# S5 loads issued by SyncE instead of GpSimd, and the tables read in two halves

## The chip, the cores and the metric

The kernel runs on one core of a Trainium2 chip, in one launch. A core has five engines that run their own instruction streams and meet at semaphores: TensorE (PE; its weight loads are shown apart as PEld), VectorE (DVE), ScalarE (ACT), GpSimd (POOL) and SyncE (SP). Transfers between HBM and the on-chip memory SBUF are issued by one of these engines and carried by 16 DMA engines that all of them share. In this kernel SyncE issues nearly all transfers, on a hardware queue; GpSimd issues some, on a software queue; ScalarE issues a few. The metric is the device time of one execution in microseconds.

## The reference

A trunk of two layers over a sequence of 1024 positions and 1024 channels, all in float32. Layer 0 has a gated DeltaNet mixer, layer 1 an S5 state-space mixer; both run beside a cross-attention of 4 heads into 256 memory tokens, and both are followed by layer norms and an MLP of 4096. The change touches only the S5 mixer of layer 1:

```python
def s5_scan(u, abar_re, abar_im, bbar_re, bbar_im, c_re, c_im):
    """h_t = Abar h_{t-1} + Bbar u_t per group; y_t = Re(C h_t). u (B,L,H) float32."""
...
def s5_mixer(x, w_in, ...):
    proj = x @ w_in
    u, xq = jnp.split(proj, [S5_DIM], axis=-1)
    ...
    y = s5_scan(u, abar_re, abar_im, bbar_re, bbar_im, c_re, c_im)
    y = y + d_skip * u
    zg = jax.nn.gelu(y)
    out = zg * jax.nn.sigmoid(zg @ w_glu + b_glu)
    return out, xq
```

There are 64 groups of 16 channels; each drives one complex state of 64 values.

## The kernel before

Large products are done in three passes of float32r halves (`mm3`, L386 to L391): every operand is split into a high part, by a cast on ScalarE, and the rest, by a subtraction on VectorE. Weights come from HBM through two buffers called raw (`load_raw`, L357; `load_split`, L362 to L370, where the issue is L359, the cast L368 and the subtraction L369).

The S5 mixer treats eight steps of time as one column, so that the scan runs over 128 columns. While layer 0's MLP runs, a side job (`s5_side`) prepares everything that doesn't depend on the activations and writes it to HBM: the rotation tables (`tabd`: a cosine table and two sine tables of opposite sign), the driving matrices (`g1d`), the reading matrices (`h1d`) and the local responses (`zd`). These stores are issued by GpSimd and stay there.

`s5_front` (L2184) then runs layer 1's mixer. It interleaves, by a string of steps, eight blocks m = 0 to 7 of eight groups each with the keys and values of the memory (wkr, wvr), the projections u (wur) and queries (wqr), the attention, and the gated unit (wgr). For a block:

- `s5_u` (L1986) projects u and writes it to `ud`; `s5_drive` loads it back as part of the tile s5t (L2040), in another layout.
- `s5_driving` (L2005), one block ahead, loads for each of two halves b of the block a matrix G1 (L2002, 256 KB) and two tables tab (L2016, 256 KB each). The first table is the cosine table, read twice by a broadcast into the lower and the upper 64 partitions. The second has one sine table in the lower 64 partitions and the other in the upper 64.
- `s5_drive` (L2034) multiplies u by G1 on TensorE (p, L2053), rotates by the tables, scans and rotates back on VectorE, with copies that swap halves on ScalarE (L2047, L2048).
- `s5_reading` (L2021) loads two matrices H1 (L2002, 256 KB each, read in runs of 512 bytes) and, through `s5_local` (L2031), the local responses M0 from `zd` (512 KB in runs of 512 bytes), into s5t, or into the tile ml for m = 7.
- `s5_read` (L2071) forms py on TensorE (L2078, L2079), applies the gelu and stores `yd` (L2082, two stores of 256 KB), which the gated unit reads again as zg (L2100).

All loads of G1, H1, tab and M0 are issued by GpSimd, 72 in all. GpSimd also computes one small power per layer norm (L512), between two VectorE instructions (L511, L519).

What sets the order: at the end of the program a planner, `settle` (L58), takes all instructions with their dependencies and puts the instructions of every engine in a fixed order, by a list schedule with estimated costs (`price`, L295), keyed to the order that TensorE's work was written in. An issue has an estimate that depends on the engine, and a transfer one that depends on its shape. Each engine then works through its own list in order, and an instruction that waits holds up all behind it on that engine. The framework also gives the transfers of the hardware queue eight semaphores in turn, so a transfer issued by SyncE waits until the one eight places before it has landed; the software queue of GpSimd has eight semaphores of its own.

Of the kernel before, what the change touches and what calls it, by code (L numbers as in the profile page):

```python
# [16 lines left out]
P = 128  # L17
# [13 lines left out]
class Trunk:  # L31
# [1967 lines left out]

    def s5_load(self, nm, tag, src):  # L2000
        t = self.tile(tag, [P, 4, P], F32, nm)
        self.nc.gpsimd.dma_start(t, src)  # L2002
        return t

    def s5_driving(self, m):  # L2005

        out = []
        for b in range(2):
            gs = slice(4 * b, 4 * b + 4)
            G1 = self.s5_load("G1", "h1", self.g1d[m, :, gs])  # L2010
            c, q = (2 * m + b) % 8, m // 4
            tabs = []
            for x in range(2):
                t = self.tile("h2", [P, 4, P], F32, "tab")
                src = self.tabd[1:3, c, q] if x else self.tabd[0, c, q].unsqueeze(0).to_broadcast([2, 64, 4, P])
                self.nc.gpsimd.dma_start(t.rearrange("p g t -> p (g t)"), src.rearrange("k p g t -> k p (g t)"))  # L2016
                tabs.append(t)
            out.append((G1, tabs))
        return out
# [7 lines left out]
    def s5_local(self, m, o):  # L2027

        M0 = o.rearrange("p (g x) -> p g x", g=8)
        z = self.zd[m]  # L2030
        self.nc.gpsimd.dma_start(M0, bass.AP(z.tensor, z.offset, [[16, 8], [8 * 240, 16], [240, 8], [1, P]]))  # L2031
        return M0

    def s5_drive(self, m, loads):  # L2034
# [447 lines left out]
```

## Time and profile before

| | us |
|---|---|
| time before, median of 3 runs | 2498.58 (2492.67 to 2499.19) |
| the profiled execution's own time | 2495.45 |
| its span, first to last instruction | 2493.7 |
| TensorE busy | 2461.7 |
| GpSimd busy | 283.7 |

The span is about 1.8 us shorter than the time of the same execution. The stage of the change lies between about 1309 us, where the load of ml is issued, and 1602 us, where the last load of H1 is. In rows of groups, a line is the line of the kernel, "out<-in" are the program's tile names without their numbers (so G is G1 and H is H1), and "xN" is the count; then come busy time, mean ns of one, and the idle time of the engine just before them with what ended it. A row of the timeline has the start in us, the length in us, engine, line, operation and tiles, and in square brackets the idle time before it. SPq is SyncE's queue of issues.

### The profile page before, as it was taken

To read this page: it belongs to the slowest core of one execution; us is meant where nothing else is said; L and a number is where in the kernel's file an instruction comes from. 1 tells how busy PE (TensorE), PEld (TensorE's weight loads), DVE (VectorE), ACT (ScalarE), POOL (GpSimd) and SP (SyncE) were. 2 spreads that over 40 slices of the span, in tenths; PEclk is the share of its full clock that TensorE was granted. 3 is DMA by queue.
4 is the path that set the end of the run, shared out by engine and by line. 5 is a ranking of instruction groups with operands and counts; after the bars stand their busy time and mean duration, and the time that the engine had idled before them with its cause. 6 is when DMAs were issued, how large, how long until landed. Compare 5 with 4: busy or idle time off the path is not lost. (4 is left out here: it accounts for less than half of the span.)

```text
span 2493.7 us, 37109 instructions
## 1 busy us (share of the span) xinstructions
PE 2461.7 (99%) x12589; PEld 2043.5 (82%) x12589; DVE 1928.7 (77%) x3629; ACT 1385.4 (56%) x3091; POOL 283.7 (11%) x405
## 2 busy tenths in 40 slices
PE   9999999999999999999999999999999999999998
PEld 7888888887787888788888888888887888888886
DVE  7776868685889987879988856683988655588777
ACT  7766677755557575554444255662466555544443
POOL 1111212110001011312120122100010000000001
PEclk9999999999999999999999999999999999999999
DMA  6544445556335665587455499874137544673422
GB/s 205 130 121 147 134 142 146 167 157 209 106 125 176 212 225 182 175 281 250 140 168 158 141 247 224 206 257 153 57 124 240 176 154 152 208 275 101 148 88 98
DMA packets 292047, 424.12 MB, mean 170 GB/s; under 512 B 120032, under 2 KB 137392, under 8 KB 291856
## 3 DMA queue, kind: packets, MB, share of 16 engines
q1 hardware_dynamic: 257520, 370.40, 46.2%
q0 software_dynamic: 31744, 46.76, 7.3%
q10 hardware_dynamic: 2592, 4.59, 0.5%
q8 instruction: 99, 1.62, 0.3%
q14 instruction: 92, 0.75, 0.1%
HBM read 285.74 MB, written 135.76 MB: 169 GB/s over the span
## 5 line engine op out<-in xcount | busy, mean ns | idle before, releaser
L389 PE MATMUL q<-wkh,hkh 128*128 128x512 f32 x784 | 306.0, 390 | 0.0
L390 PE MATMUL q<-wkl,hkh 128*128 128x512 f32 x784 | 305.7, 390 | 0.0
L391 PE MATMUL q<-wkh,hkl 128*128 128x512 f32 x784 | 305.3, 389 | 0.0
L857 ACT CAST wkh<-wr 128x512 fp32r<-128x512 f32 x168 | 104.9, 624 | 238.0 <-PE q L390 156.5
L389 PEld LDWEIGHTS q<-wkh,hkh 128*128 128x128 f32 x784 | 147.2, 188 | 31.7 <-ACT wkh L857 1.0
L391 PEld LDWEIGHTS q<-wkh,hkl 128*128 128x128 f32 x784 | 147.2, 188 | 30.5
L390 PEld LDWEIGHTS q<-wkl,hkh 128*128 128x128 f32 x784 | 147.2, 188 | 30.0
L858 DVE TENSOR_TENSOR wkl<-wr,wkh 128x512 fp32r<-128x512 f32 x168 | 115.8, 689 | 64.0 <-issue 50.9
L389 PE MATMUL wi<-xTh,wih 128*128 128x512 f32 x376 | 151.8, 404 | 1.6 <-ACT wih L368 1.6
L391 PE MATMUL wi<-xTh,wil 128*128 128x512 f32 x376 | 150.0, 399 | 0.3 <-DVE wil L369 0.3
L390 PE MATMUL wi<-xTl,wih 128*128 128x512 f32 x376 | 150.1, 399 | 0.0
L512 POOL TENSOR_TENSOR mv<-mv,mhalf 128x1 f32<-128x1 f32 x32 | 32.1, 1004 | 981.0 <-DVE mv L506 936.4
L858 DVE TENSOR_TENSOR hkl<-hr,hkh 128x512 fp32r<-128x512 f32 x196 | 134.2, 685 | 2.8 <-ACT hkh L857 2.7
L857 ACT CAST hkh<-hr 128x512 fp32r<-128x512 f32 x196 | 121.3, 619 | 4.0 <-DMA hr<-hd 4.0
L389 PE MATMUL o<-ow,ok 128*128 128x512 f32 x256 | 101.4, 396 | 1.2 <-ACT ok L1733 1.0
L391 PE MATMUL o<-ow,ok 128*128 128x512 f32 x256 | 101.5, 396 | 0.2
L390 PE MATMUL o<-ow,ok 128*128 128x512 f32 x256 | 100.2, 391 | 0.1
L850 DVE TENSOR_TENSOR y<-q,y 128x512 f32<-128x512 f32 x136 | 88.0, 683 | 0.0
L389 PEld LDWEIGHTS wi<-xTh,wih 128*128 128x128 f32 x376 | 71.2, 189 | 15.2 <-ACT wih L368 1.8
L391 PEld LDWEIGHTS wi<-xTh,wil 128*128 128x128 f32 x376 | 71.2, 189 | 14.4 <-DVE wil L369 1.0
L390 PEld LDWEIGHTS wi<-xTl,wih 128*128 128x128 f32 x376 | 71.3, 190 | 12.5
L1733 ACT CAST ok<-os 128x512 fp32r<-128x512 f32 x56 | 34.8, 623 | 54.8 <-PE o L391 41.1
(619 smaller groups left out, 7287.7 us busy)
## 6 DMA issues: line engine op xcount, KB each, us to landing
hr<-hd SPq DMA_DIRECT2D x212, 256.0 KB, 2.7
wr<-in_w_dram SPq DMA_DIRECT2D x56, 512.0 KB, 5.0
hd<-u SPq DMA_DIRECT2D x100, 256.0 KB, 2.2
w1r<-in_w_dram SPq DMA_DIRECT2D x48, 512.0 KB, 3.7
hd<-hid SPq DMA_DIRECT2D x60, 256.0 KB, 2.1
hd<-p SPq DMA_DIRECT2D x60, 256.0 KB, 2.6
w1r<-in_w_dram SPq DMA_DIRECT2D x48, 256.0 KB, 3.2
wir<-in_w_in_dram SPq DMA_DIRECT2D x23, 512.0 KB, 4.3
```

The lines of the kernel that those rows point to most:

```text
L389: mm(ps, a[0], b[0], start=start, stop=False, skip_group_check=onto)
L390: mm(ps, a[0], b[1], start=False, stop=False, skip_group_check=onto)
L391: mm(ps, a[1], b[0], start=False, stop=stop, skip_group_check=onto)
L512: nc.gpsimd.tensor_tensor(mv[:, 3:4], mv[:, 2:3], self.mhalf[:, 0:1], op=ALU.pow)
L850: V.tensor_tensor(o, bank[t], o, op=ALU.add)
L857: nc.scalar.copy(hi, s)
L858: nc.vector.tensor_tensor(lo, s, f32(hi), op=ALU.subtract)
L1733: nc.scalar.copy(hi, s)
```

## The change

`s5_load` and `s5_local` issue on SyncE instead of GpSimd. In `s5_driving`, each table is read by two transfers of 64 partitions (128 KB) on SyncE, one per half, instead of one transfer of 128 partitions (256 KB) on GpSimd: `tabd[0]` twice for the first table, `tabd[1]` and `tabd[2]` for the second. The bytes are the same. The stores of the side job, the products and the tiles are unchanged.

```diff
     def s5_load(self, nm, tag, src):
         t = self.tile(tag, [P, 4, P], F32, nm)
-        self.nc.gpsimd.dma_start(t, src)
+        self.nc.sync.dma_start(t, src)
         return t
...
             for x in range(2):
                 t = self.tile("h2", [P, 4, P], F32, "tab")
-                src = self.tabd[1:3, c, q] if x else self.tabd[0, c, q].unsqueeze(0).to_broadcast([2, 64, 4, P])
-                self.nc.gpsimd.dma_start(t.rearrange("p g t -> p (g t)"), src.rearrange("k p g t -> k p (g t)"))
+                for k in range(2):
+                    self.nc.sync.dma_start(t[64 * k:64 * k + 64], self.tabd[x * (1 + k), c, q])
                 tabs.append(t)
...
         z = self.zd[m]
-        self.nc.gpsimd.dma_start(M0, bass.AP(z.tensor, z.offset, [[16, 8], [8 * 240, 16], [240, 8], [1, P]]))
+        self.nc.sync.dma_start(M0, bass.AP(z.tensor, z.offset, [[16, 8], [8 * 240, 16], [240, 8], [1, P]]))
```

What the planner makes of it: on TensorE, VectorE and ScalarE every row stands where it stood, with the same line, operation and tile name; only the last numbers of some names, which count the program's instructions, differ. This is TensorE's order at the first products of the S5 drive (p), between two products of the memory's keys (mk), before:

```order
L390 MATMUL mk_15046<-meml_15003,wkh_15042 128x256
L391 MATMUL mk_15046<-memh_15002,wkl_15043 128x256
L2053 MATMUL p_2822_15086<-s5t_14839,G_2816_15073 128x128 x4
L2053 MATMUL p_2826_15108<-s5t_14839,G_2819_15079 128x128 x4
L389 MATMUL mk_15153<-memh_14990,wkh_15149 128x256
```

and now, at the same place of TensorE's list:

```order
L390 MATMUL mk_15046<-meml_15003,wkh_15042 128x256
L391 MATMUL mk_15046<-memh_15002,wkl_15043 128x256
L2053 MATMUL p_2822_15090<-s5t_14839,G_2816_15073 128x128 x4
L2053 MATMUL p_2826_15112<-s5t_14839,G_2819_15081 128x128 x4
L389 MATMUL mk_15161<-memh_14990,wkh_15157 128x256
```

Nothing moved there. On SyncE the loads stand between its own transfers. These are SyncE's rows from a weight to the second yd store behind it in the middle of the stage (wur and wqr are weights, ud and yd the stores, s5t<-ud the load of u), before:

```order
L359 DMA wur_15616<-in_w_in_dram 128x1024
L2082 DMA yd<-zg_15464 128x512
L2082 DMA yd<-zg_15476 128x512
L2040 DMA s5t_14839<-ud 128x1024
L359 DMA wur_15822<-in_w_in_dram 128x1024
L359 DMA wqr_16027<-in_w_in_dram 128x1024
L1997 DMA ud<-s5t_14839 128x8x128
L359 DMA wur_16062<-in_w_in_dram 128x1024
```

and now the piece from the second matrix G1 to the same last weight (its first row of G1, two yd stores and the load of M0 stand just ahead):

```order
L2002 DMA G_2899_15544<-g1d 128x512
L2002 DMA H_2902_15553<-h1d 128x4x128
L2002 DMA H_2903_15555<-h1d 128x4x128
L2040 DMA s5t_14839<-ud 128x1024
L359 DMA wur_15842<-in_w_in_dram 128x1024
L359 DMA wqr_16051<-in_w_in_dram 128x1024
L2016 DMA tab_15765<-tabd 64x512 x2
L2016 DMA tab_15770<-tabd 64x512 x2
L2016 DMA tab_15773<-tabd 64x512 x2
L2016 DMA tab_15972<-tabd 64x512 x2
L1997 DMA ud<-s5t_14839 128x8x128
L359 DMA wur_16086<-in_w_in_dram 128x1024
```

The five loads of M0, G1 and H1 come ahead of the load of u, and the eight half tables between the weights and the store of u. On GpSimd the loads stood between the powers of the layer norms (mv), here for the last three rows of the norm that ends layer 0, before:

```order
L512 TENSOR_TENSOR mv_14740<-mv_14740,mhalf 128x1
L2016 DMA tab_15077<-tabd 128x1x512
L2016 DMA tab_15081<-tabd 128x1x512
L2016 DMA tab_15083<-tabd 128x1x512
L2016 DMA tab_15132<-tabd 128x1x512
L2016 DMA tab_15134<-tabd 128x1x512
L2002 DMA G_2819_15079<-g1d 128x512
L512 TENSOR_TENSOR mv_14792<-mv_14792,mhalf 128x1
L2016 DMA tab_15138<-tabd 128x1x512
L2016 DMA tab_15140<-tabd 128x1x512
L2016 DMA tab_15343<-tabd 128x1x512
L512 TENSOR_TENSOR mv_14830<-mv_14830,mhalf 128x1
```

and now the same powers and the first of the next norm follow each other:

```order
L512 TENSOR_TENSOR mv_14740<-mv_14740,mhalf 128x1
L512 TENSOR_TENSOR mv_14792<-mv_14792,mhalf 128x1
L512 TENSOR_TENSOR mv_14830<-mv_14830,mhalf 128x1
L512 TENSOR_TENSOR mv_18512<-mv_18512,mhalf 128x1
L512 TENSOR_TENSOR mv_18566<-mv_18566,mhalf 128x1
```

GpSimd keeps no transfer in this stage; SyncE's list grows from 1299 to 1403 transfers.

## The prediction

> **What bounds the kernel now.** I read the page's busy times first, then the stage that the change touches, then the waits in it, then the DMA. The first row of the page says what the time is made of.
>
> ```profile
> PE 2461.7 (99%) x12589; PEld 2043.5 (82%) x12589; DVE 1928.7 (77%) x3629; ACT 1385.4 (56%) x3091; POOL 283.7 (11%) x405
> ```
>
> TensorE is busy for 2461.7 of 2493.7 us; only what makes it idle, or gives it more work, moves the end. The loads that change queue are issued from 1309 to 1602 us. Next comes the row of the busy times between 1400 and 1650 us, and the waits of TensorE in that stretch (in total, times, longest).
>
> ```profile
> core 0: us, PE busy (x) PEld busy (x) DVE busy (x) ACT busy (x) POOL busy (x), PEclk, DMA share, GB/s
> 1400.00:1650.00 250.00, 247.42 (x1406) 214.36 (x1405) 171.61 (x328) 136.37 (x243) 57.26 (x73) 1.00 0.86 221
> ...
> PE pv L389 <- ACT pTh L1611: 1.3, 3, 0.9
> PE mk L391 <- DVE wkl L369: 0.4, 1, 0.4
> PE wu L389 <- ACT xTh L540: 0.3, 1, 0.3
> PE pv L390 <- DVE pTl L1612: 0.2, 1, 0.2
> PE wu L390 <- DVE xTl L541: 0.2, 1, 0.2
> ```
>
> TensorE is idle for 250.00 - 247.42 = 2.6 us of 250, at full granted clock (1.00), and every named wait is for ScalarE or VectorE; none is for a transfer. So transfers that land earlier can win at most 2.6 us here, and only if one stands behind such a wait. The largest, for the attention probabilities pTh, comes after transposes of TensorE's own: no load is in it. wkl is the split of a weight that SyncE already loads.
>
> **What the change moves.** First the order of work. TensorE, VectorE and ScalarE hold the same instructions in the same order before and after, tile numbers aside, so TensorE gets no other work and no other sequence of shapes. That term is 0. Only SyncE and GpSimd change.
>
> GpSimd loses 72 transfers. These are its groups between 1300 and 1620 us (busy, mean ns of one, idle before).
>
> ```profile
> L2016 POOL DMA_DIRECT2D tab<-tabd x32 | 25.9, 815 | 106.9 <-DVE y L850 55.5 <-DVE t L2064 36.2 <-DVE r L2065 10.1
> L2002 POOL DMA_DIRECT2D H<-h1d x16 | 12.4, 793 | 4.5 <-DVE t L2064 4.5
> L2031 POOL DMA_DIRECT2D s5t<-zd x7 | 9.3, 1325 | 81.6 <-PE py L2079 56.5 <-ACT kv L1545 25.1
> L2002 POOL DMA_DIRECT2D G<-g1d x16 | 9.2, 585 | 0.0
> L2031 POOL DMA_DIRECT2D ml<-zd x1 | 1.4, 1368 | 1.1 <-DVE G1T L1925 1.1
> ```
>
> That removes 25.9 + 12.4 + 9.3 + 9.2 + 1.4 = 58.2 us from an engine that is 11% busy. It matters only where other work of GpSimd stands behind these issues: the powers of the layer norms (L512). One did, as its timeline and VectorE's wait show.
>
> ```profile
> 1411.15 3.17 POOL L2016 DMA_DIRECT2D tab<-tabd  x4 [0.57 <-PE tm L390]
> 1414.28 0.63 POOL L2002 DMA_DIRECT2D G<-g1d  x1
> 1414.88 0.61 POOL L512 TENSOR_TENSOR mv<-mv,mhalf 128x1 f32<-128x1 f32 x1
> ...
> 1413.33 0.15 DVE L511 TENSOR_SCALAR mv<-mv 128x1 f32<-128x1 f32 x1
> 1415.53 1.28 DVE L519 SCALAR_TENSOR_TENSOR y<-y,mv,gb 128x1024 f32<-128x1024 f32 x1 [0.91 <-POOL mv L512]
> ...
> 1427.01 1.04 PE L531 MATMUL xt<-ident,y 128*128 128x128 f32 x8
> 1428.34 0.49 PE L389 MATMUL wu<-xTh,wuh 128*128 128x512 f32 x1 [0.29 <-ACT xTh L540]
> ...
> 1427.21 0.59 ACT L1991 COPY s5t<-wu 128x512 f32<-128x512 f32 x1 [0.16 <-PE wu L391]
> 1427.69 1.08 ACT L540 CAST xTh<-xt 128x512 fp32r<-128x512 f32 x2
> ```
>
> VectorE was done at 1413.48; the power started 1.40 us later, behind five issues, and VectorE stood for 0.91 us. With those issues gone, this row of y is up to 0.91 us earlier. Does it reach TensorE? The next wait there, 0.29 us at 1428.34, is for the cast of xT, which ScalarE begins at 1427.69, after a copy that itself waited for TensorE's own product (0.16, PE wu). The transposes at 1427.01 had no wait. So the 0.91 us ends in VectorE's slack. I take 0; bounds 0 and -0.5 us (0.29 + 0.2, the two wu waits above).
>
> SyncE gains 104 issues: 64 half tables and 40 others. One of its issues takes 0.33 us by the wvr row below, so 104 x 0.33 = 34 us over the 300 us, and what shares the engine is only other issues. That costs nothing unless issues wait for each other, which is the real question.
>
> ```profile
> L359 SPq DMA_DIRECT2D wvr<-in_wv_dram x4: 327/330/530, 1451.1 to 1475.2; - x4
> L368 ACT CAST wvh<-wvr x4: 1047/1048/1053, 1461.0 to 1486.5; 128x1024 fp32r<-128x1024 f32 x4
> DMA to landing us min/median/max: 9.6/10.5/11.7
> ...
> L389 PE MATMUL mv<-wvh,memh x16: 389/389/476, 1470.0 to 1496.6; 128*128 128x512 f32 x16
> ...
> L2031 POOL DMA_DIRECT2D s5t<-zd x7: 1315/1324/1344, 1446.6 to 1593.1; - x7
> ```
>
> Each moved load brings its wait along, and on SyncE others queue behind it: behind a waiting zd load two yd stores, two G, two H, the load of s5t and then a weight. This is the second such place; the number in brackets is GpSimd's idle time.
>
> ```profile
> 1468.24 1.24 SPq L2082 DMA_DIRECT2D yd<-zg  x2
> 1475.20 0.33 SPq L359 DMA_DIRECT2D wvr<-in_wv_dram  x1
> ...
> 1468.93 1.32 POOL L2031 DMA_DIRECT2D s5t<-zd  x1 [7.34 <-PE py L2079]
> ```
>
> The zd load is free at 1468.9, when SyncE has its yd stores in hand, and the weight behind is due at 1475.2: eight issues of 0.33 us end by 1471.6. So the wait holds a store back by some 0.7 us (1468.93 - 1468.24) and no weight; I take 0. Without that cover a weight would be late by the whole 7.34 us. The first moved load, ml, now stands ahead of the last MLP weights at 1309 us: one issue, and 512 KB, 1.3 us at the rate found below. TensorE has no wait for a weight there (between 1300 and 1700 us it has only the five above), so 0 again.
>
> Weights lead their use: the first wvr is issued at 1451.1, cast at 1461.0, split in some 2.3 us, and used at 1470.0. That leaves 9.0 - 2.3 = 6.7 us of lead, although it took about 10 us to land. How long will loads take on SyncE's queue? The trace has no such load there, so I bound it: near, SyncE's own 256 KB loads; far, what GpSimd's queue needed.
>
> ```profile
> hr<-hd SPq DMA_DIRECT2D x212, 256.0 KB, 2.7
> tab<-tabd POOLq DMA_DIRECT2D x32, 256.0 KB, 11.9
> zg<-yd SPq DMA_DIRECT2D x16, 256.0 KB, 4.5
> ...
> GB/s 307 149 138 323 435 307 154 195 205 297 348 166 75 127 348 195 61 51 51 41 51 61 51 72 307 358 317 287 72 51 51 51 20 0 0 31 420 410 410 41
> ...
> GB/s 0 0 0 31 154 276 276 297 230 159 133 195 338 410 410 410 410 394 405 379 384 374 369 405 410 405 410 410 399 399 399 405 405 405 410 399 353 277 261 404
> ```
>
> The two rows of GB/s are slices of 0.4 us. The first spans 1364 to 1380 us, where one table and one G, 512 KB together, are alone but for two of SyncE's transfers: they end in a tail of about 51 GB/s. The second spans 1656 to 1672 us, where SyncE loads 256 KB pieces back to back at about 405. So 51 is an eighth of the full rate, and that tail, not SyncE, makes the 9 to 12 us of the moved loads. I take SyncE's rate, since the pieces are of the same 128 partitions and 2 KB rows as hr, and 4.5 us for one load (zg, short runs as H and zd have). Bounds: 2.7 and 11.9 us.
>
> The Trainium skill, page "DMA: Bandwidth & Descriptors", section "Why a DMA increments its semaphore by 16 and not by 1", says that a transfer uses the largest number of engines up to 16 that divides the outermost dimension of both sides. The old table's source has an outermost dimension of 2, so 2 engines; each half has 64, so 16. The trace agrees for the old form (51 of 405 GB/s is two engines of sixteen); no run yet shows the halves. By it the tables alone would land in SyncE's usual time, and the sum stays 0.
>
> **Sum.** 0 for order, 0 for GpSimd's relief, 0 for SyncE's issues, 0 for earlier landings: the profiled execution's own 2495.45 us stays. That execution is one of four seen (2492.67, 2495.45, 2498.58, 2499.19) and 3.1 below the median of the three runs, 2498.58; the middle of the four is (2495.45 + 2498.58) / 2 = 2497.0, and that is my time.
>
> **Rivals.**
>
> *The one queue chokes (slower).* Every transfer on SyncE's queue waits until the eighth before it has landed; GpSimd had eight places of its own. In the changed order one block of eight channel groups, from one zd load to the next, holds 20 transfers of together 5632 KB (zd 512, two yd, two G and two H of 256, s5t and ud 512 each, three weights of 512, eight half tables of 128). The row of s5t<-zd above gives the period: (1593.1 - 1446.6) / 6 = 24.4 us. Eight in flight and 20 per 24.4 us allow a latency of 8 x 24.4 / 20 = 9.8 us. Fixed time is about 2.7 - 0.26 / 0.405 = 2.1 us; eight mean pieces of 0.288 MB are 2.3 MB, 5.7 us at 405 GB/s, 7.8 us in all: it holds, by 2 us. It breaks below 2.3 / (9.8 - 2.1) = 0.30 MB per us.
>
> ```profile
> q1 hardware_dynamic: 257520, 370.40, 46.2%
> q0 software_dynamic: 31744, 46.76, 7.3%
> ```
>
> For it: over the whole run the hardware queue moved 370.40 MB in 46.2% of the span, 321 GB/s, not far above 300; GpSimd's queue 46.76 MB in 7.3%, 257 GB/s. If the moved patterns hold their 257 on the new queue, eight take 2.1 + 8.9 = 11.0 us, a period 27.5 us, 3.1 more, seven times 22 us, less the lead of 6.7: +15 us, **2512**. TensorE would then wait at wu and wq for casts whose weights are late. Against it: those averages contain two queues sharing engines, and the stretch 1400 to 1650 needs only 221 GB/s. Chance 0.08.
>
> The Trainium skill, same page, section "Queues, rings and completion order", says that each engine takes turns between the queues that have work, packet by packet; on one queue the weights lose their own turn and stand behind all tables issued before them. That speaks for this rival. The trace shows the sharing, not the single queue: the wvr loads took 10.5 us beside GpSimd's, so which of the two is worse stays open until the run.
>
> *All waits of the stage go (faster).* If late loads delayed ScalarE and VectorE in ways the waits don't name, up to 2.6 us go: 2497.0 - 2.6 = **2494.4**. Against it: the five waits above follow from the order of casts. Chance 0.12; it is still within 0.3%.
>
> *It does not do what it says.* The planner could have put the loads elsewhere; the rows of the order settle that it has not, so I give it no chance of its own.
>
> **How the numbers follow.** 0.3% of this kernel, 7.5 us, is about what a measurement can tell from no change. Forecast "no change" 0.75 at 2497.0; faster rival 0.12; slower rival 0.08; the remaining 0.05 is for a gain above 7.5 us by something that I don't see, since it would need three times TensorE's idle time here. So faster 0.05, same 0.75 + 0.12 = 0.87, slower 0.08. The range starts at the lowest run less the idle time, 2492.67 - 2.6 = 2490, and ends at the highest plus one period's loss of the slower rival, 2499.19 + 3.1 = about 2503; it leaves out the choked queue and the unseen gain.
>
> **What would show it.** Right: the tables land in 3 to 6 us instead of 11.9, TensorE's busy time between 1400 and 1650 stays within 3 us of 247.42, its waits are still for pTh, wkl and xTh, and VectorE's 0.91 us wait for L512 is gone. Wrong: waits of TensorE for wuh, wqh or G, ScalarE's casts waiting for landings, or SyncE waiting in sum for landings rather than for engines; or a stage whose TensorE work is shorter, which nothing here explains.

## The result and the profile after

| | before | after | ratio, 95% interval |
|---|---|---|---|
| first comparison, 19 runs each, us | 2496.64 (2492.67 to 2501.96) | 2491.74 (2488.68 to 2493.66) | 0.9982 (0.9976 to 0.9988) |
| second, 23 and 11 runs | 2497.47 (2493.89 to 2503.25) | 2493.14 (2491.06 to 2495.74) | 0.9979 (0.9971 to 0.9988) |
| third, 34 and 11 runs | 2499.76 (2493.43 to 2505.36) | 2493.70 (2492.49 to 2497.73) | 0.9979 (0.9969 to 0.9988) |

The changed kernel is 4 to 6 us faster, about 0.2%. That is less than the 0.3% that the prediction counts as a difference, but three comparisons agree on it, so it is real. The ranges differ too: those of before are about twice as wide (9.3, 9.4 and 11.9 us against 5.0, 4.7 and 5.2; only the first two are of equally many runs). The kernel before loses something that isn't lost in every execution.

The first profile after shows nothing of that. Its busy times and DMA queues, from the page (queue, packets, MB, share of 16 engines):

```profile
PE 2460.2 (99%) x12589; PEld 2042.3 (82%) x12589; DVE 1928.3 (77%) x3629; ACT 1383.7 (56%) x3091; POOL 224.0 (9%) x333
...
q1 hardware_dynamic: 281648, 391.38, 49.5%
q0 software_dynamic: 10112, 25.64, 3.3%
```

The stage from 1400 to 1650 us by busy times (columns as before), and below it TensorE's waits in it:

```profile
1400.00:1650.00 250.00, 247.46 (x1406) 214.45 (x1406) 171.65 (x327) 135.94 (x242) 3.05 (x4) 1.00 0.78 220
```

```profile
PE pv L389 <- ACT pTh L1611: 1.1, 2, 0.9
PE mk L391 <- DVE wkl L369: 0.4, 1, 0.4
PE wu L389 <- ACT xTh L540: 0.3, 1, 0.3
```

TensorE was busy for 247.42 us there and is now busy for 247.46, with the same waits. GpSimd went from 57.26 us to 3.05, and the DMA engines' share fell from 0.86 to 0.78 at the same 220 GB/s. By these two profiles the stage is worth nothing. Yet the profiled execution of before ran in 2495.45 us, 1.2 below the median of its 19 runs, and that of after in 2493.66, the highest of its 19: a good execution of the one was compared with a poor one of the other. So the question of the study: what does the kernel before lose in its other executions, and which part of the change stops it?

To place a loss, the table of stretches below takes the matmuls of two traces one by one (12589 in each), since TensorE's order is the same: how much later than in the first profile after does TensorE get from one matmul to another? That is worked out from the traces, and given in us by stretches of time.

### The profile page after: what moved, and what is told of

It reads as the page before. It is cut to its first block, busy times and chain, and to the rows that moved or that the text cites. A ratio compares the mean times of both kernels' runs of the same rounds, so it can differ in the third digit from the quotient of the medians.

```text
span 2491.9 us, 37103 instructions
## 1 busy us (share of the span) xinstructions
PE 2460.2 (99%) x12589; PEld 2042.3 (82%) x12589; DVE 1928.3 (77%) x3629; ACT 1383.7 (56%) x3091; POOL 224.0 (9%) x333
## 3 DMA queue, kind: packets, MB, share of 16 engines
q1 hardware_dynamic: 281648, 391.38, 49.5%
```

## The experiments

**One part at a time.** Four kernels separate the tables from the other loads, the halving from the queue.

Only the tables move (G1, H1 and the zd loads stay on GpSimd):

```
-  src = self.tabd[1:3, c, q] if x else self.tabd[0, c, q].unsqueeze(0).to_broadcast([2, 64, 4, P])
-  self.nc.gpsimd.dma_start(t.rearrange("p g t -> p (g t)"), src.rearrange("k p g t -> k p (g t)"))
+  for k in range(2):
+      self.nc.sync.dma_start(t[64 * k:64 * k + 64], self.tabd[x * (1 + k), c, q])
```

> Only the tables go in halves of 64 partitions by SyncE's queue; G1, H1 and the zd loads stay on GpSimd's (40 transfers of 256 to 512 KB there, 64 halves on SyncE). TensorE's, VectorE's and ScalarE's order is that of both kernels. The change as a whole measured 0.9982 of before, -4.9 us. Theory A, the software queue costs time per transfer wherever it is used: 32 of 72 transfers leave it, so about -2.2 us (0.9991). Theory B, the tables' source of outer dimension two is what costs: the whole -4.9 us (0.9980 to 0.9985). Theory C, what the prediction on record has (none of these loads is waited for, the terms are nothing, and the measured gain comes by chance of timing elsewhere): 1.0000 within 0.0006 here.

Measured: 2495.82 us, 0.9987 (0.9978 to 0.9996).

The complement, G1, H1 and zd:

```
-  self.nc.gpsimd.dma_start(t, src)
+  self.nc.sync.dma_start(t, src)
...
-  self.nc.gpsimd.dma_start(M0, bass.AP(z.tensor, z.offset, [[16, 8], [8 * 240, 16], [240, 8], [1, P]]))
+  self.nc.sync.dma_start(M0, bass.AP(z.tensor, z.offset, [[16, 8], [8 * 240, 16], [240, 8], [1, P]]))
```

> The complement: G1, H1 and the zd loads (40 transfers) go by SyncE's queue, the 32 tables stay on GpSimd's, each in one transfer. Orders of the three compute engines as before. Theory A (price per software transfer): 40 of 72 leave, about -2.7 us (0.9989). Theory B (the tables' shape): nothing, 1.0000. Theory C: 1.0000 within 0.0006.

Measured: 2496.59 us, 0.9990 (0.9980 to 0.9999).

The tables in halves, but everything on GpSimd's queue:

```
-  self.nc.gpsimd.dma_start(t.rearrange("p g t -> p (g t)"), src.rearrange("k p g t -> k p (g t)"))
+  for k in range(2):
+      self.nc.gpsimd.dma_start(t[64 * k:64 * k + 64], self.tabd[x * (1 + k), c, q])
```

> All stays on GpSimd's queue, but each table comes in two transfers of 64 partitions, so GpSimd issues 104 instead of 72. The planner then moves four rows of VectorE's list and two of ScalarE's near 1400 to 1430 us by a few places; else the order is the same. Theory A (price per software transfer, -4.9 us for 72): 32 more cost +2.2 us (1.0009). Theory B (the tables' shape is the cost): -4.9 us (0.998). Theory C: 1.0000, since GpSimd has room for 32 issues of 0.8 us, except for its power per layer norm at 1414 us, which may be late by one issue more (+0.3 us).

Measured: 2495.88 us, 0.9987 (0.9976 to 0.9999).

Everything on SyncE's queue, but each table whole:

```
-  self.nc.gpsimd.dma_start(t.rearrange("p g t -> p (g t)"), src.rearrange("k p g t -> k p (g t)"))
+  self.nc.sync.dma_start(t.rearrange("p g t -> p (g t)"), src.rearrange("k p g t -> k p (g t)"))
```

> All 72 loads go by SyncE's queue, but each table in one transfer of 128 partitions with the source as before. Orders of the three compute engines as before. Theory A (leaving the software queue): as the change, 0.9976 to 0.9988. Theory B (shape): 1.0000, the tables landing as late as before (near 12 us); with eight transfers in flight on SyncE such late landings would show as waits of SyncE's queue, and the kernel could even be slower. Theory C: 1.0000 within 0.0006.

Measured: 2581.99 us, 1.0329 (1.0314 to 1.0345): 83 us slower.

What follows. Of the last, theory B alone allowed that it could be slower, and none expected so much. From its trace, the group of the table issues (duration ns min/median/max), and in the second fence TensorE's largest waits from 1400 to 1700 us:

```profile
L2016 SPq DMA_DIRECT2D tab<-tabd x32: 484/2936/7113, 1365.6 to 1666.4; - x32
```

```profile
PE wu L389 <- ACT xTh L540: 30.9, 1, 30.9
PE wu L389 <- ACT wuh L368: 11.2, 1, 11.2
PE wq L389 <- ACT wqh L368: 11.1, 1, 11.1
PE py L2078 <- DMA s5t<-zd: 9.5, 3, 6.5
PE py L2079 <- DMA H<-h1d: 9.0, 4, 2.6
```

A whole table holds SyncE for 2.9 us in the median, up to 7.1, in the issue alone; a half in the changed kernel holds it for 0.47. Everything else in SyncE's line, weights first, stands behind it. (Not all of the 83 us are these waits: TensorE's granted clock is 0.87 there from 1400 to 1700 us.) The halving is not a refinement of the move; it is what makes the move possible.

The other three all come out a little below 1, and the totals decide little between the theories: A misses e3_split (1.0009), B misses e2_rest by a hair (1.0000), and the band of C (down to 0.9994) reaches into all three intervals. Their traces are more telling: two show waits of TensorE that neither of the first two profiles has, of e2_rest and then of e3_split, both between 1440 and 1530 us:

```profile
PE wq L391 <- DVE wql L369: 1.6, 1, 1.6
```

```profile
PE wu L389 <- ACT wuh L368: 1.2, 1, 1.2
PE wq L391 <- DVE wql L369: 1.1, 1, 1.1
PE wu L391 <- DVE wul L369: 1.1, 2, 0.6
```

These are waits for casts and splits of weights (wur, wqr) that SyncE loads in the middle of S5's stage. So a new theory, D: in the kernel before, too, these weights come late in some executions, and the profile of before was of one where they just came in time.

**More executions of both kernels.** Copies without an edit; each brings a profile of its own.

> The kernel before, unchanged, timed against itself: ratio 1.000, interval about 0.001 to either side. Its profile is a second execution of the kernel before. Theory D (the weights wqr and wur of S5's stage land late in some executions, because S5's loads on GpSimd's queue, tables on two engines or not, share the transfer engines with them; the profile on which the prediction stands was an execution without the stall): of three further executions of the kernel before at least one shows TensorE waiting 1 to 6 us in all for wuh, wul, wqh or wql between 1480 and 1515 us, as the executions of e2_rest (1.6) and e3_split (3.4) did. Theory C (chance of timing elsewhere): no such wait in any of them, TensorE's idle time from 1400 to 1650 us stays at 2.6 us.

> A third execution of the kernel before with a profile. Theory D: TensorE's idle time between 1400 and 1650 us varies from execution to execution by some us, and in the same us as the landing of wur and wqr issued at 1480 to 1500 us; theory C: it stays at 2.6 us.

> A fourth execution of the kernel before with a profile; theories as for the third.

> The changed kernel, unchanged, on the same chip as the copies of the kernel before. Theory D: 0.9975 to 0.9990, a narrower spread of its times than before's, and in its profile TensorE's busy time from 1400 to 1650 us within 0.5 us of the first profile's 247.46, with wqr issued at 1489 us landing in under 6 us. Theory C: the ratio nearer to 1 than 0.9988, or TensorE's gain found ahead of 1400 us.

Measured: b1_again 2497.34 us, 1.000 (0.999 to 1.001); b2_again 2498.02 and b3_again 2501.17, one run each; a1_again 0.9979 (second row of the first table). TensorE's waits in b3_again between 1440 and 1530 us, and in the second fence its row of busy times from 1500 to 1520 us:

```profile
PE wu L389 <- ACT wuh L368: 1.8, 1, 1.8
PE wu L391 <- DVE wul L369: 1.3, 2, 0.8
PE py L2079 <- DMA H<-h1d: 0.5, 1, 0.5
```

```profile
1500.00:1520.00 20.00, 17.71 (x77) 13.86 (x76) 10.01 (x19) 5.31 (x10) 3.23 (x4) 1.00 0.79 231
```

In these 20 us TensorE begins 77 matmuls, against 114 in the row of the changed kernel:

```profile
1500.00:1520.00 20.00, 20.00 (x114) 17.45 (x114) 8.10 (x15) 7.79 (x13) 0.00 (x0) 1.00 0.89 233
```

By stretches, in us later than the first profile after:

| execution | start to 1400 | 1400 to 1515 | 1515 to 1740 | 1740 to 1775 | 1775 to the last matmul | behind it |
|---|---|---|---|---|---|---|
| before, first profile | -0.3 | 0.1 | 0.1 | 0.8 | 0.7 | 0.5 |
| b1_again | -1.0 | 1.5 | 0.0 | 0.9 | 0.2 | 0.6 |
| b2_again | 1.4 | 1.9 | 0.0 | 0.8 | -0.3 | 0.5 |
| b3_again | 1.1 | 5.0 | 0.1 | 1.0 | -0.2 | 0.6 |
| a1_again | 0.2 | 0.0 | 0.0 | 0.0 | -0.7 | -0.1 |
| a2_again (below) | -0.3 | 0.0 | 0.0 | 0.7 | 0.0 | 0.0 |

Up to 1400 us the kernels do the same, and the numbers scatter around zero for both. Between 1400 and 1515 us before loses 0.1 to 5.0 us, 2.1 in the mean, and the changed kernel nothing in any of three. Theory D holds; theory C falls. Of the 8.5 us that the four lose in this stretch, 5.5 come where TensorE reaches one weight wur, near 1500 us, and 1.1 at the wur before it. Two waits for H1, which GpSimd's own queue brings, make 1.3, and a wait for xT near 1430 us the rest. Two more losses, near 1758 us and behind the last matmul, are taken up below.

Why the weight is late can be read in SyncE's and GpSimd's issues. First b3_again, SyncE's and then GpSimd's timeline (start, length, engine, line, tiles):

```profile
1493.72 0.38 SPq L1997 DMA_DIRECT2D ud<-s5t  x1
1494.49 0.82 SPq L359 DMA_DIRECT2D wur<-in_w_in_dram  x1
```

```profile
1493.68 1.31 POOL L2031 DMA_DIRECT2D s5t<-zd  x1 [7.14 <-PE py L2079]
1494.99 1.15 POOL L2002 DMA_DIRECT2D G<-g1d  x2
1496.10 1.55 POOL L2002 DMA_DIRECT2D H<-h1d  x2
```

and what became of that wur: who waited for it, and how long it took to land:

```profile
  ACT wuh L368: 6.8, 1
...
DMA to landing us min/median/max: 12.4/12.4/12.4
```

The same piece of the changed kernel:

```profile
1489.99 0.38 SPq L1997 DMA_DIRECT2D ud<-s5t  x1
1490.77 0.33 SPq L359 DMA_DIRECT2D wur<-in_w_in_dram  x1
1491.19 1.31 SPq L2082 DMA_DIRECT2D yd<-zg  x1
1492.59 0.63 SPq L2031 DMA_DIRECT2D s5t<-zd  x1
1493.32 3.86 SPq L2082 DMA_DIRECT2D yd<-zg  x1
1497.22 0.92 SPq L2002 DMA_DIRECT2D G<-g1d  x2
```

Before, GpSimd issues zd, G and H as soon as it may, in the same microseconds as SyncE's wur, and both queues share the transfer engines: wur takes 12.4 us, and ScalarE stands for 6.8 us until it has it. After, there is one line, in which wur stands ahead of zd, G and H; G is issued 6.4 us behind it. wur then lands 5.9 us after its issue, worked out from the semaphore events. Over all traces this wur lands at 1500.6, 1501.3, 1504.2 and 1506.9 us in the four executions of before, and at 1496.6, 1496.9 and 1496.4 us in the three of after. From issue to landing that is 11.8, 11.9, 11.9 and 12.4 us against 5.9, 6.1 and 6.7.

So the four executions of before hardly differ in how long this load takes, and they still lose 0.1 to 5.0 us. What differs is when it goes out. In the three that lose most, ScalarE's cast of the weight before (wvr) waits 4.5 to 4.9 us for that weight's landing; the copy of u, the store ud and wur in SyncE's line all come behind this cast. In the first profile the same cast waited for TensorE (3.3 us), and wur was issued early enough.

It isn't this one load alone. From issue to landing, the 22 weights that SyncE loads between 1400 and 1650 us take 7.2 to 8.0 us in the median in the four executions of before, and 4.7 to 4.8 in the three of after (from the semaphore events). Not every weight gains, and the order in the line shows in which ones do: in the first profile after, the three wvr that SyncE issues behind zd, G and H take 9.9 to 11.7 us, and the one ahead of them 5.4. In the first profile before, the four took 9.6 to 11.7.

**What is scarce, and which part.** Four more runs. In the first all loads stay on GpSimd's queue, but a table transfer brings a quarter of its bytes:

```
-  self.nc.gpsimd.dma_start(t.rearrange("p g t -> p (g t)"), src.rearrange("k p g t -> k p (g t)"))
+  self.nc.gpsimd.dma_start(t[:, 0:1].rearrange("p g t -> p (g t)"), src[:, :, 0:1].rearrange("k p g t -> k p (g t)"))
...
-  V.tensor_tensor(t1, p1, tab[0], op=M)
+  V.tensor_tensor(t1, p1, tab[0][:, 0:1].to_broadcast([P, 4, P]), op=M)
...
+  if i.outs[0].bass_ap.tensor.name.startswith("tab_"):
+      size, k = 262.144, 2048
```

(the same for the other three products; the last two lines keep the planner's estimates).

> The kernel before with all its loads on GpSimd's queue, but each table transfer brings only the first of the four groups (64 KB instead of 256 KB, runs of 512 bytes; the products read that group for all four, so the output is another). The estimates are left as they were, so all five engines keep their order; 6.3 MB of the stage's traffic go, the number of software transfers and of packets doesn't. Theory D (the loads share saturated transfer engines between 1460 and 1500 us and make the weights late): DMA share there falls below 0.95, no wait of TensorE for wuh, wul, wqh, wql, ratio 0.9980 to 0.9992, while the 0.8 us step at the output projection near 1758 us stays. Theory A (price per software transfer, whatever its size): 1.000, with waits for weights as in the copies of the kernel before.

Measured: 2494.89 us, 0.9979 (0.9971 to 0.9988), the whole gain of the change. Its row of busy times from 1480 to 1500 us, and in the second fence TensorE's only wait from 1440 to 1530 us (its lines stand two further down):

```profile
1480.00:1500.00 20.00, 20.00 (x114) 17.49 (x113) 11.90 (x18) 10.06 (x15) 5.52 (x7) 1.00 0.96 226
```

```profile
PE mk L393 <- DVE wkl L371: 0.4, 1, 0.4
```

With the same number of software transfers, and whatever GpSimd's issues cost still there, the waits for weights are gone. So a price per software transfer (theory A) doesn't explain them; what those transfers take from the transfer engines does. The 22 weights of the stage land in 4.9 us in the median here, as they do after the change. The step near 1758 us is still 0.6 us. The DMA share of the row (it adds up the packets' times, so it can pass 1) is 0.96, a hair above the 0.95 that was expected, against 1.08 in the same row of the first profile of before:

```profile
1480.00:1500.00 20.00, 20.00 (x115) 17.45 (x114) 10.33 (x16) 8.54 (x13) 5.54 (x7) 1.00 1.08 259
```

The second and third are repeats side by side: the tables alone, and the full change.

> Again only the tables in halves on SyncE's queue, now beside the full change on one chip. If the tables alone are what made the weights late: ratio that of a2_again within 0.0005, no wait for weights in its profile. If G1, H1 and the zd loads on GpSimd's queue have a share: between 1 and a2_again's, about 0.9990, and waits for weights in some executions.

> The changed kernel as it is, as the yardstick of this call: 0.9976 to 0.9988, and a third profile with no wait for wuh, wul, wqh or wql between 1480 and 1515 us and no step near 1758 us.

Measured: e1_again 2495.79 us, 0.9986 (0.9977 to 0.9996); a2_again 2493.70, 0.9979 (0.9969 to 0.9988). From e1_again, TensorE's largest wait between 1440 and 1530 us:

```profile
PE py L2079 <- DMA H<-h1d: 1.1, 1, 1.1
```

The tables alone bring some two thirds, twice; in e1_again the wait is not for a weight but for an H1 that is still on GpSimd's queue, and e1_tabs, profiled in its fastest run, lost only 0.1 us in the stage. The other loads alone bring a half (e2_rest). Each part lightens the same crowd, so the parts don't add up to the whole. The intervals of e1_again and a2_again overlap; that both parts are needed rests on e1_again's wait for H and on e2_rest's wait for wql more than on the totals. e3_split stays unclear in its total: its profile, of a run 3.4 us above its median, loses 4.8 us in the stage, but its time is below that of before, and some rows of VectorE and ScalarE had moved near 1400 to 1430 us. Its trace is worth a comparison all the same, since it differs from the changed kernel in the queue and not in the form of the tables. The rows of busy times from 1480 to 1500 us, of e3_split and of the changed kernel:

```profile
1480.00:1500.00 20.00, 18.86 (x108) 16.22 (x107) 10.38 (x17) 8.91 (x15) 7.26 (x12) 1.00 0.87 228
```

```profile
1480.00:1500.00 20.00, 20.00 (x114) 17.49 (x113) 11.93 (x19) 9.96 (x15) 0.00 (x0) 1.00 0.87 234
```

The transfer engines are equally busy (0.87), yet wqr and wur take 10.2 and 11.4 us to land in e3_split, and 4.8 and 5.9 in the changed kernel. So the mean share doesn't tell late weights from early ones; there, with this one profile of e3_split, the queue does. Over the whole stage the form of the tables matters more: the median landing of the 22 weights is 5.0 us in e3_split, 5.0 and 5.7 in e1_tabs and e1_again, but 6.9 in e2_rest, which keeps the whole tables.

**The second place, near 1758 us.** There all four executions of before lose 0.8 to 1.0 us. No load of S5 is near. But the output projection's first loads (os, 16 transfers back to back from about 1729 us on) land later in them; by the semaphore events the fourth takes 5.6 to 5.9 us, and 5.1 in the first two profiles after. All 16 stand in SyncE's line, which the change makes longer ahead of them. The test: 64 transfers of 4 bytes on that line, 400 to 700 us earlier, nothing else.

```
+  for k in range(8):
+      nc = self.nc
+      nc.sync.dma_start(self.junk[0:1, 8 * m + k:8 * m + k + 1], self.g1d[m, 0:1, 7, 0:1])
...
+  if i.outs[0].bass_ap.tensor.name.startswith("junk"):
+      return 0.0, 0.0, 0.0
```

> The kernel before with 64 transfers of 4 bytes more on SyncE's queue, eight at a time, between 1000 and 1320 us, read by nobody; all engines keep their order. Near 1758 us TensorE loses 0.8 to 1.0 us at the output projection in all four executions of the kernel before, and nothing in the changed kernel, where the burst of os loads at 1730 us lands about 1 us earlier (fourth load 4.7 instead of 5.8 us). Theory O1 (the place of the burst in SyncE's sequence of transfers decides, by the count of those ahead of it: 64 more, as with e1_tabs): the step is gone, the fourth os load lands in 4.7 us, ratio about 0.9997. Theory O2 (it is the path on which the tables came): the step stays at 0.8 us, ratio 1.000. Either way the waits for weights near 1500 us stay, by theory D.

Measured: 2498.84 us, 0.9999 (0.9990 to 1.0009). The loss near 1758 us is gone (-0.1 us), and the fourth os load takes 4.8 us. TensorE's weight loads with a wait before them, in the first profile of before and in x_count, from 1745 to 1775 us (lines two further down in the second):

```profile
1756.99 0.19 PEld L389 LDWEIGHTS o<-ow,ok 128*128 128x128 f32 x1 [0.49 <-ACT ow L1733]
1757.53 0.19 PEld L391 LDWEIGHTS o<-ow,ok 128*128 128x128 f32 x1 [0.24 <-DVE ok L1683]
1758.13 0.19 PEld L389 LDWEIGHTS o<-ow,ok 128*128 128x128 f32 x1 [0.41 <-DVE y L1683]
1765.95 0.19 PEld L390 LDWEIGHTS o<-ow,ok 128*128 128x128 f32 x1 [0.20 <-DVE ow L1683]
1766.55 0.19 PEld L391 LDWEIGHTS o<-ow,ok 128*128 128x128 f32 x1 [0.41 <-DVE ok L1683]
```

```profile
1773.95 0.19 PEld L392 LDWEIGHTS o<-ow,ok 128*128 128x128 f32 x1 [0.22 <-DVE ow L1685]
1774.55 0.19 PEld L393 LDWEIGHTS o<-ow,ok 128*128 128x128 f32 x1 [0.41 <-DVE ok L1685]
```

The first three waits, on which the loss rests, are missing in x_count. The test rules out theory O2: 64 transfers that carry no table take the loss away. But the number of transfers ahead doesn't decide alone, as O1 has it: e2_rest, with 40 more, lost 0.4 us there, and a2_again, with 104 more, 0.7. What holds in all traces is the landing: where the fourth os load takes 4.7 to 5.1 us nothing is lost, at 5.3 (e2_rest) 0.4 us, and at 5.6 to 5.9 us 0.6 to 1.0 us (a2_again: 5.8). What makes it land sooner stays open.

x_count also gave the worst stage of all: 7.2 us lost between 1400 and 1515 us, with TensorE waiting for the same weight,

```profile
PE wu L391 <- ACT wuh L370: 3.3, 1, 3.3
```

as theory D says of a kernel that has all of S5's loads on GpSimd's queue. About 1.5 of the 7.2 us come right behind this wait, while TensorE's granted clock is lower (0.91, third number from the end):

```profile
1500.00:1520.00 20.00, 15.96 (x62) 12.16 (x61) 10.23 (x19) 5.18 (x8) 3.23 (x4) 0.91 0.77 221
```

**A third place, behind the last matmul.** The last store of the output, issued by ScalarE 6.8 us after the start of the last matmul in both kernels, takes 2.75 to 2.87 us to land in the four executions of before and 2.22 to 2.29 in the three of after. That is the last column of the table of stretches. In x_count the end comes as early behind the last matmul as after the change (9.9 us, against 10.6 to 10.8 before and 10.1 to 10.2 after), so it isn't the path of the tables here either; but e3_split, which adds nothing to SyncE's line, ends equally early. The cause stays open.

## Why the prediction was right, and where its reasons failed

*Time and class held; the reason for no change did not.* 2491.74 us lies in the range, and the gain is under the 0.3% that the prediction's classes go by. But the prediction's sum is 0, and the change wins 4 to 6 us, more than the 2.6 us that it gave as the most that could be won. The measured time is 5.3 us below the forecast of 2497.0; that the class held is luck as far as the mechanism goes: the gain came by a way that the sum has at 0, and happened to be small.

*Order of work: 0.* Held; TensorE's 12589 matmuls follow each other alike, and TensorE's time to 1400 us scatters around zero.

*GpSimd's relief: VectorE's 0.91 us for the power would go, worth 0.* The zero fits, the reading half: in the profile after the five issues ahead of the power are gone, but the power itself took 1.40 us instead of 0.61, and VectorE still waits 0.44:

```profile
1413.93 1.40 POOL L512 TENSOR_TENSOR mv<-mv,mhalf 128x1 f32<-128x1 f32 x1 [5.77 <-DVE mv L511]
...
1415.37 1.28 DVE L519 SCALAR_TENSOR_TENSOR y<-y,mv,gb 128x1024 f32<-128x1024 f32 x1 [0.44 <-POOL mv L512]
```

*SyncE's 104 issues and the waits that moved with them: 0.* Held by outcome. The zd load's wait for py holds up no weight, and SyncE's waits for places are there, as these rows of its waits from 1400 to 1650 us show (in total, times, longest), without harm to TensorE:

```profile
SPq L2016 <- DMA s5t<-ud: 6.4, 5, 2.0
SPq L2016 <- DMA H<-h1d: 5.9, 10, 1.7
SPq L2016 <- DMA wvr<-in_wv_dram: 5.2, 3, 1.9
```

```profile
SPq L359 <- DMA s5t<-zd: 3.1, 2, 1.8
```

The prediction would have counted it as a sign against it if SyncE waited more for landings than for engines; it waits some 43 us for landings and 109 for engines there. Most of the waits for landings hold back tables, which have time; the last row is of weights, and TensorE shows no wait for them.

*Earlier landings: 0, since TensorE waits for no transfer there.* **This is the step that failed.** The halves do land in 2.6 to 9.5 us, 5.8 in the median (from the semaphore events), where 3 to 6 had been expected. But what counts isn't their own landing; it is that of the weights beside them. "TensorE is idle for 2.6 us" was read from one execution, and in that one the late wur still came in time: it was cast at 1500.7 us, 4 us after ScalarE was ready for it. The row that showed it was in reach, among ScalarE's waits in the profile of before:

```profile
ACT wuh L368 <- DMA wur<-in_w_in_dram: 4.0, 1, 4.0
```

The prediction named casts that wait for landings as a sign of being wrong, but this one was already there in the kernel before; and the changed kernel has them too (7.3 us for wvr from 1400 to 1650 us), where TensorE loses nothing. So the sign doesn't separate the two. And the prediction's own quoted landing of wvr, 9.6 to 11.7 us, said the same of the other weights. In the other three executions that lead did not suffice. The bound of 2.6 us was thus a bound for that execution, not for the kernel.

*The rival of the choked queue* was right in what it would do, and e4_whole shows it: one queue in which slow transfers stand before weights, with TensorE waiting at wu and wq, at +83 us. It is another way of choking, though: the issues themselves hold SyncE, by 2.9 us each, while its waits for landings from 1400 to 1650 us come to some 16 us only. The rival's size (+15) was for moved loads at the software queue's rate; the halves never came to that.

The Trainium skill, page "DMA: Bandwidth & Descriptors", section "Queues, rings and completion order", says that engines take turns between the queues that have work; the prediction took from it that weights on one queue would lose their turn. The traces agree with the sharing (12.4 us for wur beside GpSimd's loads), and show another consequence here: in the one line, where the planner's order has wur ahead of zd, G and H, wur lands in 5.9 us. The wvr loads that stand behind zd, G and H there take 9.9 to 11.7 us, but TensorE has time for these.

*The account.* The mean spans of the four executions of before and the three of after that were profiled differ by 4.0 us (2495.9 against 2491.9). Of these, 2.1 us are lost from 1400 to 1515 us, some 0.6 near 1758 us, and 0.6 behind the last matmul: 3.3 in all. The other 0.7 us lie half before 1400 us and half between 1775 us and the last matmul, where single executions of either kernel scatter, and aren't explained. The medians of all runs differ by 4.3 to 6.1 us; four profiled executions are too few for the mean of a loss that goes from 0 to 5 us (x_count, which issues S5's loads as before does, lost 7.2).

## What to carry to other kernels

One profile shows the waits of one execution. Where the times of a kernel scatter by more than the effect, take its lowest and its highest run as a warning, look for loads that land late but just in time, and read how much lead is left there rather than the wait alone. Moving loads to the queue that carries the weights can help, since their order then sets who goes first; but only if no transfer in that line is slow to issue, so first change the form of those that are, as the halving does here.

## What the runs showed of the hardware

- A whole 256 KB table with its source of outer dimension two held SyncE's issue for 2.9 us in the median (e4_whole), a half for 0.47 us. On GpSimd's queue the whole one took 0.82 us to issue. The form isn't all that holds an issue: in the changed kernel one store of yd took 3.86 us.
- The form of the tables costs the transfer engines more than the queue does. The 21 MB that change queue made up 7.3 - 3.3 = 4.0% of 16 engines' span with whole tables on the software queue, 6.8 - 3.3 = 3.5% with halves on the same queue (e3_split), and 49.5 - 46.2 = 3.3% with halves on the hardware queue.
- GpSimd's power of 128 numbers took 0.61 us right behind an issue, and 1.40 to 1.42 us at the same place in the three profiles after, behind 5.8 us of idling. The idling isn't the reason, since the power before it took 0.55 us behind 5.9 us of idling. It did run beside VectorE's subtraction of wul (1413.71 to 1414.93 us), which in the profile before had ended (1414.61) when the power began (1414.88). No run tests this.
- 64 transfers of 4 bytes on a queue changed the landing of a burst 400 to 700 us later by 1.0 us (5.8 to 4.8). What of the queue's state does that stays open.
- Behind a wait of TensorE of 3.3 us the granted clock of the 20 us around it was 0.91 (x_count); around a wait of 1.8 us it was 1.00 (b3_again).
